# A two-layer diffusion backbone on one core: first-stage statistics, modulation and weight tiles loaded, merged and ordered anew

## The chip, the cores and the metric

The kernel runs on one core of a Trainium2 chip. The metric is the device time of one execution in microseconds, as a median of several. TensorE (PE) does the matrix products and PEld is its weight load; VectorE is DVE, ScalarE is ACT, and SP is the queue that issues every transfer from HBM.

## What is computed

The reference is a backbone of two layers over 512 latent tokens and 256 context tokens with 1024 features. Each layer normalises every token, modulates it, mixes tokens and adds the result under a gate. Only the entry of layer 0 matters here:

```python
def _rms(x):
    return x * lax.rsqrt(jnp.mean(x * x, axis=-1, keepdims=True) + NORM_EPS)

def modulation(cond, mod_w, mod_b):
    m = jax.nn.silu(cond) @ mod_w + mod_b
    return jnp.split(m, 3, axis=-1)     # shift, scale, gate

# a layer: h = _rms(x) * norm_g * (1 + scale) + shift, for latents by c, for context by c_ctx
u = h @ w_in                            # 1024 x 4096, first product of the mixer
```

All arithmetic is in float32. A product of two float32 matrices is made of three passes over halves of reduced mantissa (hi and lo).

## The kernel before, in words

Features lie on partitions, in eight tiles of 128 (k = 0 to 7); tokens lie along the free axis, 256 of the context first (`acc_c`) and 512 latents after them (`acc_l`), 768 in all. A feature tile of the modulated input h is a pair (`hh`, `hl`), a weight tile of 128 by 1024 is split into (`whi`, `wlo`), on ACT for hi and on DVE for lo (`split_w`, L85 to L93). `mm3` (L75 to L78) issues the three products lo by hi, hi by hi and hi by lo. `mm_in` (L279) makes one output tile of 128 channels: for each k six matmuls of 384 tokens, three in each half.

The first stage (L246 to L381) has this order in the program:

- Transfers, all on SP, in this order: the constants (L60); x in four pieces of two feature tiles, context before latents in each (L247, L248); then in turn the first three weight tiles and the modulation weights of f = 0, 1, 2, with a weight tile ahead of each (L291 to L296). A modulation tile is 1 MB and has four buffers; f = 3 to 7 are fetched in the loop (L374).
- 48 products of ones keep PE at work until the statistics come (`warm_up`, L302).
- Statistics: ACT squares all eight feature tiles (L306, L307), DVE adds them up one by one (L309). For each block of 128 tokens a matmul with one moving column sums over partitions (`token_sums`, L198), apart for context and latents; ACT takes the square root and DVE the reciprocal (L204, L205). `token_spread` (L209) multiplies by the identity so that each partition holds 1/rms of every token in PSUM, and ACT copies that to `rstd` in SBUF (L319).
- Modulation of one feature tile f: `mod_mm(f)` is 16 small matmuls (L328) and a copy of the rows to SBUF (L332); `mod_out(f)` sums the rows with a matmul (L172) and DVE makes shift and gain (L338, L343). `mod_mm(0)` is held back behind the last spread (L353).
- `normed(k)` is x by `rstd` on DVE (L348, L349). `make_h` makes `hh` on ACT (L223), the same in full precision (`tmp`, on DVE L225 or on ACT L227), and `hl` as their difference on DVE (L228).
- The loop over k: make h for k, then `mod_mm(k+1)` and `normed(k+1)`, then `mm_in` for k of three output tiles (two of the branch that is convolved, one gate), with `mod_out(k+1)` after the first of them. So the modulation runs one feature tile ahead. At k = 0 the second and third weight tiles are split whole (`take(3, 2)`, L366), after h of k = 0; at k = 3 a softplus of 40 columns is computed.

Program order is a priority, not a fixed order: a scheduler at compile time puts the instructions of each engine in order by its own estimate, and `issue_after` forces one instruction behind another. At run time every engine takes its instructions in that fixed order. After the stage come sixteen iterations of layer 0 and then layer 1; the change does not touch them.

An fp32 matmul that is not of reduced mantissa appears as two instructions in the trace: 50 products of ones are 100 rows, and one `mod_mm` is 32.

Of the kernel before, what the change touches and what calls it, by code (L numbers as in the profile page):

```python
# [7 lines left out]
F32 = mybir.dt.float32  # L8
# [35 lines left out]
def backbone(ctx: ExitStack, tc: tile.TileContext, xT, vec, trig, lru_mod_sc, lru_mod_gt, lru_w_in, lru_w_g, lru_w_out,  # L44
# [171 lines left out]
    def cut(pair, a, b):  # L216
        return [t[:, a:b] for t in pair]
# [16 lines left out]
    with ExitStack() as l0:  # L234
# [14 lines left out]
        nc.scalar.activation(out=cond[:, :, 0:2], in_=vt[:, V_COND:V_COND + 16].rearrange("p (k t) -> p k t", t=2),  # L249
                             func=AF.Silu)  # L250
        segs = ((0, NC), (NC, NT))
# [27 lines left out]
        def mm_in(w, ps, ks=range(KD)):  # L279
            for k in ks:  # L280
                wk = [t[:, k * P:(k + 1) * P] for t in w]
                for a, b in halves:
                    mm3(ps[:, 128 + a:128 + b], wk, cut(hs[k], a, b), k == 0, k == KD - 1)

        with tc.tile_pool(name="mp", bufs=4) as mp, tc.tile_pool(name="mp1", bufs=1) as mp1:
# [16 lines left out]
            warm_up(48)  # L302
            ssum = e("ssum")
            for k in range(KD):
# [6 lines left out]
            parts = [(ssum[:, a:b], slots[1][:, 512 * i:512 * i + 4], (slots[0], slots[2])[i][:, 512:512 + b - a], rstd[:, a:b], b - a)  # L311
                     for i, (a, b) in enumerate(segs)]
# [10 lines left out]
            def mod_mm(f):  # L323
                raw = mraw.pop(f)
                for k in range(KD):
# [20 lines left out]
            def normed(k):  # L346
                t = e("nx")
                nc.vector.tensor_tensor(out=t[:, 0:NC], in0=acc_c[:, k, :], in1=rstd[:, 0:NC], op=ALU.mult)  # L348
                nc.vector.tensor_tensor(out=t[:, NC:NT], in0=acc_l[:, k, :], in1=rstd[:, NC:NT], op=ALU.mult)  # L349
                return t  # L350

            split_to(0)
            with tc.issue_after(spread.ins):  # L353
                rows = mod_mm(0)
            mod_out(0, rows)
            warm_up(4)
            us[0], gps, us[1] = slots[0], slots[1], slots[2]
            nx = normed(0)
            for k in range(KD):
# [4 lines left out]
                if k == 0:  # L364
                    with tc.issue_after(last_lo[0].ins), tc.issue_after(last_hi[0].ins):
                        w3 = take(3, 2)  # L366
# [5 lines left out]
                if k + 1 < KD:  # L372
                    if k + 3 < KD:
                        mraw[k + 3] = mod_load(k + 3)  # L374
                    rows = mod_mm(k + 1)
                    nx = normed(k + 1)
                mm_in(w3[0], us[0], [k])
                if k + 1 < KD:
                    mod_out(k + 1, rows)
                mm_in(w3[1], gps, [k])  # L380
                mm_in(w3[2], us[1], [k])  # L381
# [576 lines left out]
```

## Time and profile before

| | us |
|---|---|
| median of 3 executions | 1082.06 |
| lowest and highest | 1081.18, 1083.04 |
| the profiled execution, its own time | 1082.99 |
| its span from the first to the last instruction | 1081.2 |
| PE, DVE and ACT busy in the span | 1058.2, 706.8, 573.0 |
| granted TensorE clock, mean | 0.994 |

Times in rows are counted from the start of the span. In a row of the timeline the first number is the start and the second the duration, both in microseconds; several equal instructions in a row are merged (x12), and what stands in brackets is the idle time of the engine before it and what ended it. A clock of 1.00 is 2.4 GHz and 0.50 is 1.2 GHz. The ends of matmuls are modelled: where they follow each other, the distance of their starts is the better price.

### The profile page before, as it was taken

What the parts mean: (1) busy time and instruction counts of PE and PEld (TensorE: products, weight loads), DVE (VectorE), ACT (ScalarE), POOL (GpSimd) and SP (SyncE); (2) the same over time, 40 slices, a digit from 0 to 9 for tenths busy, and PEclk for the clock granted to TensorE, in tenths of its full rate; (3) what the DMA queues carried; (4) which work ended last, traced back from release to release, by engine and by line L of the source; (5) the groups of instructions that cost most, each with busy time, mean ns of one, the idle gap of its engine ahead of it and who ended that gap; (6) DMA issues with size and microseconds to landing.
All of it is one profiled execution on the core that took longest, in us unless ns stands there. A gap on an engine that the chain in (4) does not pass through costs nothing.

```text
span 1081.2 us, 15148 instructions
## 1 busy us (share of the span) xinstructions
PE 1058.2 (98%) x6284; PEld 965.0 (89%) x6284; DVE 706.8 (65%) x991; ACT 573.0 (53%) x745; POOL 1.1 (0%) x5
## 2 busy tenths in 40 slices
PE   8999999999999999999999999999999999999996
PEld 7898789999999999998889988899888988889886
DVE  4777667886788777878989755462555525544256
ACT  5557778766687468788366343132432324222254
POOL 0000000000000000000000000000000000000000
PEclk9999999999999999999999999999999999999998
DMA  9524653221222121222113512311122112231102
GB/s 361 220 73 154 205 169 115 69 71 66 69 69 65 53 67 41 78 71 77 68 40 118 195 39 78 98 59 39 59 77 79 59 39 63 74 98 41 39 1 79
DMA packets 29045, 95.56 MB, mean 88 GB/s; under 512 B 2992, under 2 KB 6192, under 8 KB 27952
## 3 DMA queue, kind: packets, MB, share of 16 engines
q1 hardware_dynamic: 28976, 94.59, 26.8%
q8 instruction: 49, 0.80, 0.3%
q14 instruction: 20, 0.16, 0.0%
HBM read 92.48 MB, written 2.10 MB: 87 GB/s over the span
## 4 chain that ended last, share of the span: by engine, by line
PE 64%; ACT 7%; DVE 6%; issue 2%; DVEq 0%
PE ps L76 21%; PE ps L77 21%; PE ps L78 21%; ACT g L468 1%; ACT a L467 1%; DVE xl L264 1%; DVE g L486 1%; ACT q L470 1%; ACT L483 1%; ACT L467 1%; ACT g L452 1%; DVE q L499 1%; DVE q L492 1%; DVE q L498 1%; ACT q L483 1%
## 5 line engine op out<-in xcount | busy, mean ns | idle before, releaser
L76 PE MATMUL ps<-hl,whi 128*128 128x384 f32 (+2 forms) x816 | 286.3, 351 | 1.6 <-DVE hl L228 1.4
L78 PE MATMUL ps<-hh,wlo 128*128 128x384 f32 (+2 forms) x816 | 283.3, 347 | 0.1
L77 PE MATMUL ps<-hh,whi 128*128 128x384 f32 (+2 forms) x816 | 282.9, 347 | 0.0
L91 ACT ACTIVATE whi<-wraw 128x1024 fp32r<-128x1024 f32 (+1 forms) x125 | 125.0, 1001 | 216.9 <-PE ps L77 174.0
L92 DVE TENSOR_TENSOR wlo<-wraw,whi 128x1024 fp32r<-128x1024 f32 (+1 forms) x126 | 145.1, 1153 | 95.6 <-ACT whi L91 75.0
L76 PEld LDWEIGHTS ps<-hl,whi 128*128 128x128 f32 x816 | 153.5, 188 | 18.8 <-issue 3.5
L78 PEld LDWEIGHTS ps<-hh,wlo 128*128 128x128 f32 x816 | 153.4, 188 | 11.0 <-issue 0.8
L77 PEld LDWEIGHTS ps<-hh,whi 128*128 128x128 f32 x816 | 153.5, 188 | 10.3 <-issue 1.0
L76 PE MATMUL ps<-yl,whi 128*128 128x384 f32 (+2 forms) x416 | 143.6, 345 | 3.9 <-DVE yl L501 2.1
L78 PE MATMUL ps<-yh,wlo 128*128 128x384 f32 (+2 forms) x416 | 142.6, 343 | 0.0
L77 PE MATMUL ps<-yh,whi 128*128 128x384 f32 (+2 forms) x416 | 142.5, 343 | 0.0
L77 PE MATMUL ps<-whi,hh 128*128 128x256 f32 x384 | 108.7, 283 | 0.0
L78 PE MATMUL ps<-whi,hl 128*128 128x256 f32 x384 | 108.6, 283 | 0.0
L76 PE MATMUL ps<-wlo,hh 128*128 128x256 f32 x384 | 108.6, 283 | 0.0
L76 PEld LDWEIGHTS ps<-yl,whi 128*128 128x128 f32 x416 | 78.3, 188 | 11.7 <-DVE yl L501 2.9
L78 PEld LDWEIGHTS ps<-yh,wlo 128*128 128x128 f32 x416 | 78.3, 188 | 5.7
L77 PEld LDWEIGHTS ps<-yh,whi 128*128 128x128 f32 x416 | 78.3, 188 | 5.5
L77 PEld LDWEIGHTS ps<-whi,hh 128*128 128x128 f32 x384 | 73.7, 192 | 0.3
L76 PEld LDWEIGHTS ps<-wlo,hh 128*128 128x128 f32 x384 | 73.7, 192 | 0.3
L78 PEld LDWEIGHTS ps<-whi,hl 128*128 128x128 f32 x384 | 73.7, 192 | 0.0
L452 ACT ACTIVATE g<-ps,vt 128x768 f32<-128x768 f32 x64 | 56.2, 897 | 9.1 <-PE ps L78 8.9
L264 DVE SCALAR_TENSOR_TENSOR xl<-ps,vt,xl 128x255 f32<-128x255 f32 (+1 forms) x96 | 54.3, 605 | 0.0
(190 smaller groups left out, 1553.9 us busy)
## 6 DMA issues: line engine op xcount, KB each, us to landing
wraw<-in_ret_w_in_dram SPq DMA_DIRECT2D x48, 512.0 KB, 3.5
wraw<-in_lru_w_in_dram SPq DMA_DIRECT2D x32, 512.0 KB, 3.7
mraw<-in_lru_mod_sc_dram SPq DMA_DIRECT2D x8, 1024.0 KB, 8.8
wraw<-in_ret_mod_w_dram SPq DMA_DIRECT2D x16, 512.0 KB, 4.8
wraw<-in_lru_w_out_dram SPq DMA_DIRECT2D x16, 512.0 KB, 3.5
wraw<-in_ret_w_out_dram SPq DMA_DIRECT2D x16, 512.0 KB, 3.6
wraw<-in_lru_w_g_dram SPq DMA_DIRECT2D x16, 256.0 KB, 2.7
wraw<-in_lru_mod_gt_dram SPq DMA_DIRECT2D x8, 512.0 KB, 4.2
```

What stands on the lines that cost most here:

```text
L76: nc.tensor.matmul(ps, lhsT=lhs[0], rhs=rhs[1], start=first, stop=False)
L77: nc.tensor.matmul(ps, lhsT=lhs[0], rhs=rhs[0], start=False, stop=False)
L78: return nc.tensor.matmul(ps, lhsT=lhs[1], rhs=rhs[0], start=False, stop=last)
L91: nc.scalar.activation(out=hi, in_=raw, func=AF.Copy)
L92: nc.vector.tensor_tensor(out=lo, in0=raw, in1=hi.bitcast(F32), op=ALU.subtract)
L264: nc.vector.scalar_tensor_tensor(out=t[:, o0:o1], in0=u[:, o0 + sh:o1 + sh], scalar=cw[j], in1=t[:, o0:o1], op0=ALU.mult, op1=ALU.add)
L452: nc.scalar.activation(out=t, in_=ps[:, 128:896], func=AF.Sigmoid, bias=vt[:, boff:boff + 1])
L467: nc.scalar.activation(out=a, in_=r, func=AF.Exp, scale=sneg[:, d * CT + c:d * CT + c + 1])
L468: nc.scalar.activation(out=r, in_=r, func=AF.Tanh, scale=spos[:, d * CT + c:d * CT + c + 1])
L470: nc.scalar.activation(out=q, in_=a, func=AF.Square)
L483: nc.scalar.activation(out=q, in_=q, func=AF.Sqrt)
L486: nc.vector.tensor_tensor(out=i, in0=i, in1=q, op=ALU.mult)
```

## The change

1. Transfers: the modulation weights f = 0 come before the first weight tile, f = 1 before the second and third, and f = 2 and 3 after them. Of the last piece of x the latents come before the context. The weights of f + 4 are fetched as soon as `mod_mm(f)` is issued.
2. A square root of one element is put behind the SiLU at the start, so that its table is loaded there.
3. Statistics: only six feature tiles are added up on DVE. The latents of tiles 6 and 7 are squared on ACT, their context on DVE, and both are summed by PE directly: 18 one-column matmuls (6 for the six tiles, 4 + 4 for the latents of tiles 6 and 7, 2 + 2 for their context) and one matmul by zeros that opens the sum, where 6 were before. All six token blocks lie in one 6-column tile, so there is one square root and one reciprocal. `mod_mm(0)` stands between the two spreads in the program and is no longer held back by an `issue_after`. 44 products of ones, none later.
4. `normed(0)` reads the spread from PSUM; the copies to `rstd` come after h of k = 0.
5. The three weight tiles are split in two parts, the first 128 columns (all that k = 0 needs) and the other 896; the heads early, the rests among the matmuls of k = 0.
6. The modulation and `make_h` run two feature tiles ahead of the matmuls.

Cut to its core:

```diff
-            nc.sync.dma_start(out=acc_c[:, k:k + 2, :], in_=xv[:, k:k + 2, 0:NC])
-            nc.sync.dma_start(out=acc_l[:, k:k + 2, :], in_=xv[:, k:k + 2, NC:NT])
+            for a, sl in ((acc_c, slice(0, NC)), (acc_l, slice(NC, NT)))[::-1 if k == 6 else 1]:
+                nc.sync.dma_start(out=a[:, k:k + 2, :], in_=xv[:, k:k + 2, sl])
...
+        with tc.issue_after(silu.ins):
+            nc.scalar.activation(out=warm, in_=eps, func=AF.Sqrt)
...
+            mraw = {0: mod_load(0)}
             fetch_to(0)
-            mraw = {0: mod_load(0)}
-            fetch_to(1)
             mraw[1] = mod_load(1)
             fetch_to(2)
-            mraw[2] = mod_load(2)
+            mraw[2], mraw[3] = mod_load(2), mod_load(3)
...
-            warm_up(48)
+            warm_up(44)
...
-            for k in range(KD):
+            for k in range(6):
...
+            sq6, sq7 = e("sq6"), e("sq7")
+            for k, sq in ((6, sq6), (7, sq7)):
+                nc.scalar.activation(out=sq[:, NC:NT], in_=acc_l[:, k, :], func=AF.Square)
+            for k, sq in ((6, sq6), (7, sq7)):
+                nc.vector.tensor_tensor(out=sq[:, 0:NC], in0=acc_c[:, k, :], in1=acc_c[:, k, :], op=ALU.mult)
...
-            for sq, pt, _, _, n in parts:
-                token_sums(pt, sq, n)
-            warm_up(2)
-            rts = [token_rstd(pt, n, D)[0] for _, pt, _, _, n in parts]
-            for rt, (_, _, ps, rs, n) in zip(rts, parts):
-                spread = token_spread(ps, rt, n)
-                nc.scalar.activation(out=rs, in_=ps, func=AF.Copy)
+            tok = slots[1][:, 0:6]
+            parts = [(ssum, t) for t in range(6)] + [(sq, t) for sq in (sq6, sq7) for t in range(2, 6)]
+            parts += [(sq, t) for sq in (sq6, sq7) for t in range(2)]
+            none = mp1.tile([P, 6], F32, name="none")
+            nc.vector.memset(none, 0.0)
+            nc.tensor.matmul(tok, lhsT=ones, rhs=none, start=True, stop=False)
+            for n, (sq, t) in enumerate(parts):
+                nc.tensor.matmul(tok[:, t:t + 1], lhsT=sq[:, t * P:(t + 1) * P], rhs=ones[:, 0:1], start=False,
+                                 stop=n == len(parts) - 1)
+            rt = mp1.tile([P, 6], F32, name="rt6")
+            nc.scalar.activation(out=rt, in_=tok, func=AF.Sqrt, scale=1.0 / D, bias=eps)
+            nc.vector.reciprocal(out=rt, in_=rt)
+            rsp = [slots[0][:, 512:512 + NC], slots[2][:, 512:1024]]
...
+            def w_part(i, sl):
+                if i == len(w3):
+                    w3.append((wp.tile([P, 1024], F32R, tag="whi", name="whi"), wp.tile([P, 1024], F32R, tag="wlo", name="wlo")))
+                raw, (hi, lo) = raws[i][0], w3[i]
+                nc.scalar.activation(out=hi[:, sl], in_=raw[:, sl], func=AF.Copy)
+                nc.vector.tensor_tensor(out=lo[:, sl], in0=raw[:, sl], in1=hi[:, sl].bitcast(F32), op=ALU.subtract)
...
+            head, rest = slice(0, P), slice(P, 1024)
+            rows = {}
+            token_spread(rsp[0], rt[:, 0:2], NC)
+            rows[0] = mod_mm(0)
+            w_part(0, head)
+            token_spread(rsp[1], rt[:, 2:6], NL)
+            nx = normed(0, rsp)
+            mod_out(0, rows[0])
+            rows[1] = mod_mm(1)
+            us[0], gps, us[1] = slots[0], slots[1], slots[2]
+            dst = [us[0], gps, us[1]]
+            make_hs(0, nx)
+            for a, b, ps in ((NC, NT, rsp[1]), (0, NC, rsp[0])):
+                with tc.issue_after(last_hi[0].ins):
+                    nc.scalar.activation(out=rstd[:, a:b], in_=ps, func=AF.Copy)
+            with tc.issue_after(last_lo[0].ins):
+                w_part(1, head)
+                nx = normed(1)
+                w_part(0, rest)
+            mark = mm_in(w3[0], dst[0], [0])
+            with tc.issue_after(mark.ins):
+                mod_out(1, rows[1])
+            make_hs(1, nx)
+            nx = normed(2)
+            mm_in(w3[1], dst[1], [0])
+            w_part(2, head)
+            mm_in(w3[2], dst[2], [0])
+            w_part(1, rest)
+            rows[2] = mod_mm(2)
+            w_part(2, rest)
+            for k in range(1, KD):
+                if 3 <= k < 6:
+                    rows[k + 2] = mod_mm(k + 2)
+                mm_in(w3[0], dst[0], [k])
+                if k == 1:
+                    mod_out(2, rows[2])
+                    make_hs(2, nx)
+                    nx = normed(3)
+                elif k == 2:
+                    mod_out(3, rows[3])
+                    make_hs(3, nx)
+                    nx = normed(4)
+                elif k < 6:
+                    mod_out(k + 2, rows[k + 2])
+                mm_in(w3[1], dst[1], [k])
+                if k == 2:
+                    rows[4] = mod_mm(4)
+                mm_in(w3[2], dst[2], [k])
+                if k == 1:
+                    rows[3] = mod_mm(3)
+                elif k == 2:
+                    mod_out(4, rows[4])
+                if 2 <= k < 6:
+                    make_hs(k + 2, nx)
+                    if k < 5:
+                        nx = normed(k + 3)
...
```

## Rows read from the trace of the kernel before

**Rows 1.** Busy time, share of the span and instructions of each engine

```profile
PE 1058.2 (98%) x6284; PEld 965.0 (89%) x6284; DVE 706.8 (65%) x991; ACT 573.0 (53%) x745; POOL 1.1 (0%) x5
```

**Rows 2.** Busy time by stretch: start:end, length, busy (instructions), PEclk, DMA share, GB/s

```profile
18.00:19.00 1.00, 0.52 (x2) 0.53 (x3) 0.33 (x2) 0.38 (x2) 0.00 (x0) 0.50 0.97 401
...
15.00:25.90 10.90, 7.80 (x98) 6.90 (x98) 6.43 (x15) 6.12 (x11) 0.00 (x0) 0.84 1.01 416
```

**Rows 3.** Timeline of ACT and DVE up to the end of the statistics

```profile
3.36 1.28 ACT L249 ACT_TABLE_LOAD   x1 [3.36 <-DMA vt<-in_vec_dram]
4.65 0.22 ACT L249 ACTIVATE cond<-vt 128x16 f32<-128x16 f32 x1
...
7.36 0.63 ACT L307 ACTIVATE ssum<-acc_l 128x512 f32<-128x512 f32 x1 [1.88 <-DMA acc_l<-in_xT_dram]
...
13.64 1.15 ACT L307 ACTIVATE sq<-acc_l 128x512 f32<-128x512 f32 x2 [0.33 <-DMA acc_l<-in_xT_dram]
...
10.10 6.27 DVE L309 TENSOR_TENSOR ssum<-ssum,sq 128x768 f32<-128x768 f32 x6 [0.60 <-ACT sq L307]
```

**Rows 4.** Timeline of PE and its weight loads up to the first matmul of the stage

```profile
1.05 12.98 PE L300 MATMUL ps<-ones 128*128 128x128 f32 x100 [1.05 <-DVE ones L64]
16.42 1.41 PEld L198 LDWEIGHTS ps<-ones,ssum 128*128 128x128 f32 x12 [2.59 <-DVE ssum L309]
...
18.48 2.93 PE L209 MATMUL ps<-vt,rt 128*128 128x128 f32 x12 [0.55 <-DVE rt L205]
21.34 1.08 PE L328 MATMUL ps<-mraw,cond 128*32 128x128 f32 x32
22.35 0.71 PE L300 MATMUL ps<-ones 128*128 128x128 f32 x4
...
25.91 0.45 PE L76 MATMUL ps<-hl,whi 128*128 128x384 f32 x1 [1.13 <-DVE hl L228]
```

**Rows 5.** Timeline of ACT and DVE from the sums to the first h

```profile
17.96 0.42 ACT L204 ACTIVATE rt<-ps,eps 128x2 f32<-128x2 f32 x2 [0.69 <-PE ps L198]
...
21.45 0.60 ACT L319 ACTIVATE rstd<-ps 128x512 f32<-128x512 f32 x1 [1.32 <-PE ps L209]
22.07 0.69 DVE L349 TENSOR_TENSOR nx<-acc_l,rstd 128x512 f32<-128x512 f32 x1 [1.50 <-ACT rstd L319]
...
23.45 0.23 DVE L343 TENSOR_SCALAR g<-m,vt 128x2 f32<-128x2 f32 x1
...
23.71 1.31 ACT L223 ACTIVATE hh<-nx,m,g 128x256 fp32r<-128x256 f32 x2 [0.94 <-DVE g L343]
...
25.17 0.68 DVE L228 TENSOR_TENSOR hl<-tmp,hh 128x512 fp32r<-128x512 f32 x1
...
26.37 1.22 DVE L92 TENSOR_TENSOR wlo<-wraw,whi 128x1024 fp32r<-128x1024 f32 x1
```

**Rows 6.** Periods of k = 0, 3, 4, 5: length, PE busy, PEclk, DMA

```profile
25.90:31.30 5.40, 5.03 (x52) 1.00 0.88 363
40.75:46.02 5.27, 4.87 (x55) 1.00 0.78 307
46.02:50.37 4.35, 4.35 (x53) 1.00 0.00 1
50.37:55.10 4.73, 4.65 (x56) 1.00 0.34 115
```

**Rows 7.** Waits of the weight load from 26 to 62 us: total, times, longest

```profile
PEld ps L76 <- DVE hl L228: 3.2, 6, 1.4
```

**Rows 8.** Row sum of f = 1, one-column sums at the end, normalising in layer 1

```profile
27.08 0.28 PE L172 MATMUL ps<-vt,rows 128*128 128x4 f32 x2
...
1063.80 0.50 PE L198 MATMUL ps<-ones,fs 128*128 128x1 f32 x4
1064.16 0.36 PE L76 MATMUL ps<-yl,whi 128*128 128x256 f32 x1
...
L538 DVE TENSOR_TENSOR nx<-acc_l,ps 128x512 f32<-128x512 f32 x8 | 5.5, 681 | 0.0
```

More of the change, by code (lines that the diff above doesn't have):

```diff
@@ L246, in backbone @@
         for k in range(0, KD, 2):
-            nc.sync.dma_start(out=acc_c[:, k:k + 2, :], in_=xv[:, k:k + 2, 0:NC])
-            nc.sync.dma_start(out=acc_l[:, k:k + 2, :], in_=xv[:, k:k + 2, NC:NT])
-        nc.scalar.activation(out=cond[:, :, 0:2], in_=vt[:, V_COND:V_COND + 16].rearrange("p (k t) -> p k t", t=2),
+            for a, sl in ((acc_c, slice(0, NC)), (acc_l, slice(NC, NT)))[::-1 if k == 6 else 1]:
+                nc.sync.dma_start(out=a[:, k:k + 2, :], in_=xv[:, k:k + 2, sl])
+        silu = nc.scalar.activation(out=cond[:, :, 0:2], in_=vt[:, V_COND:V_COND + 16].rearrange("p (k t) -> p k t", t=2),
                              func=AF.Silu)
+        with tc.issue_after(silu.ins):
+            nc.scalar.activation(out=warm, in_=eps, func=AF.Sqrt)
         segs = ((0, NC), (NC, NT))
@@ L282, in mm_in @@
                 for a, b in halves:
-                    mm3(ps[:, 128 + a:128 + b], wk, cut(hs[k], a, b), k == 0, k == KD - 1)
+                    m = mm3(ps[:, 128 + a:128 + b], wk, cut(hs[k], a, b), k == 0, k == KD - 1)
+            return m
         with tc.tile_pool(name="mp", bufs=4) as mp, tc.tile_pool(name="mp1", bufs=1) as mp1:
@@ L309, in backbone @@
                     nc.vector.tensor_tensor(out=ssum, in0=ssum, in1=sq, op=ALU.add)
-            rstd = mp1.tile([P, NT], F32, name="rstd")
-            parts = [(ssum[:, a:b], slots[1][:, 512 * i:512 * i + 4], (slots[0], slots[2])[i][:, 512:512 + b - a], rstd[:, a:b], b - a)
-                     for i, (a, b) in enumerate(segs)]
-            for sq, pt, _, _, n in parts:
-                token_sums(pt, sq, n)
-            warm_up(2)
-            rts = [token_rstd(pt, n, D)[0] for _, pt, _, _, n in parts]
-            for rt, (_, _, ps, rs, n) in zip(rts, parts):
-                spread = token_spread(ps, rt, n)
-                nc.scalar.activation(out=rs, in_=ps, func=AF.Copy)
+            sq6, sq7 = e("sq6"), e("sq7")
[3 more added lines that the diff above has]
+                nc.vector.tensor_tensor(out=sq[:, 0:NC], in0=acc_c[:, k, :], in1=acc_c[:, k, :], op=ALU.mult)
+            rstd = mp1.tile([P, NT], F32, name="rstd")
+            tok = slots[1][:, 0:6]
[11 more added lines that the diff above has]
+            rsp = [slots[0][:, 512:512 + NC], slots[2][:, 512:1024]]
             bank = [slots[3][:, 0:512], slots[3][:, 512:1024]]
@@ L324, in mod_mm, with mod_mm_ @@
                 raw = mraw.pop(f)
+                try:
+                    return mod_mm_(f, raw)
+                finally:
+                    if f + 4 < KD:
+                        mraw[f + 4] = mod_load(f + 4)
+            def mod_mm_(f, raw):
                 for k in range(KD):
@@ L344, in mod_out, with normed, make_hs @@
                                                scalar2=vt[:, V_LG + f:V_LG + f + 1], op0=ALU.add, op1=ALU.mult)
-            def normed(k):
+            def normed(k, rs=(rstd[:, 0:NC], rstd[:, NC:NT])):
                 t = e("nx")
-                nc.vector.tensor_tensor(out=t[:, 0:NC], in0=acc_c[:, k, :], in1=rstd[:, 0:NC], op=ALU.mult)
-                nc.vector.tensor_tensor(out=t[:, NC:NT], in0=acc_l[:, k, :], in1=rstd[:, NC:NT], op=ALU.mult)
-                return t
[L352 to L359, printed above, removed]
+                nc.vector.tensor_tensor(out=t[:, 0:NC], in0=acc_c[:, k, :], in1=rs[0], op=ALU.mult)
+                nc.vector.tensor_tensor(out=t[:, NC:NT], in0=acc_l[:, k, :], in1=rs[1], op=ALU.mult)
+                return t
+            w3 = []
+            def w_part(i, sl):
[4 more added lines that the diff above has]
+                nc.vector.tensor_tensor(out=lo[:, sl], in0=raw[:, sl], in1=hi[:, sl].bitcast(F32), op=ALU.subtract)
+            def make_hs(k, nx):
                 tmp = e("tmp")
@@ L363, in backbone @@
                 make_h(cut(hs[k], NC, NT), NL, nx[:, NC:NT], g0[:, k, 0:1], m0[:, k, 0:1], tmp[:, NC:NT], k == 0)
-                if k == 0:
-                    with tc.issue_after(last_lo[0].ins), tc.issue_after(last_hi[0].ins):
-                        w3 = take(3, 2)
+            head, rest = slice(0, P), slice(P, 1024)
[4 more added lines that the diff above has]
+            token_spread(rsp[1], rt[:, 2:6], NL)
@@ L371, in backbone @@
                         nc.vector.tensor_scalar(out=spos, in0=sp[:, 0:32], scalar1=LRU_C, scalar2=None, op0=ALU.mult)
[L372 to L381, printed above, removed]
+            ready += w3
+            raws[0:3] = [None] * 3
+            pos[0] = 3
         yp = l0.enter_context(tc.tile_pool(name="yp", bufs=7, reuse_waits="tile"))
```

## The prediction

> **What bounds the kernel now.** I read the share of busy time first: PE is busy in 98% of the span [rows 1], so time can only come out of places where PE waits or does extra work. Then the busy time by stretch: from 15 to 25.9 us PE is busy for 7.8 of 10.9 us, and the mean clock is 0.84, with half clock from 18 us [rows 2]. The change lies there and in the 34 us behind it. The timeline of PE gives the head: ones until 14.03, a wait of 2.4 us for the sums, sums, spreads, modulation, and the first matmul of the stage at 25.91 [rows 4]. Everything later hangs on that matmul, so what the head and the stage give up moves the rest of the program.
>
> The chain of the head, step by step: six more additions on DVE run back to back from 10.10 to 16.37, 1.045 us each, while the last squares are ready at 14.79 [rows 3]; so DVE, not HBM, sets the end of the statistics. The 12 one-column instructions take 1.41 us, 0.1175 each, as long as their weight loads [rows 4]; square root at 17.96, spread from 18.48 [rows 4, 5]. The spread takes 12 instructions from 18.48 to 21.34, 0.24 each, at half clock [rows 2, 4]. Then the copy to SBUF (0.60), the latents' product (0.69), and with the gain ready at 23.68 the 2.2 us until h is there [rows 5].
>
> In the stage one period of k is 4.35 us where nothing waits (k = 4: busy 4.35) and no row sum falls in it [rows 6]; a row sum adds 0.28 [rows 8]. Period 0 took 5.40 instead of 4.63 (0.77 lost), period 3 with two row sums 5.27 instead of 4.91 (0.36), period 5 4.73 instead of 4.63 (0.10) [rows 6, 7]. Two more like period 5, and the sum is 1.4 us that running ahead can recover; of the 3.2 us that weight loads wait for h [rows 7], most is under a preceding matmul.
>
> **The change part by part.**
>
> *Transfers.* x is all there at about 13.6 [rows 3]. At 416 GB/s [rows 2] a 1 MB tile takes 2.5 us and a weight tile 1.25: by this estimate modulation 0 lands at 16.2, weight tile 0 at 17.4, modulation 1 at 19.9, weights 1 and 2 at 21.2 and 22.4, modulation 2 and 3 at 25 and 27.5. Nothing below asks for one earlier. On SP the tiles f = 4 to 7 wait for `mod_mm` 0 to 3, all over by 33 us, so the weight tile queued behind them is not later than now. Latents before context in the last piece: squares of latents ready by 14.2 instead of 14.79. Worth nothing by themselves.
>
> *Table of the square root.* It moves from the head, where it hid under the sums, to 4.87 us. In the row the first ACTIVATE starts 0.01 us after a load of 1.28 [rows 3], so squares start 1.5 us later, at 6.4, and the two pairs that could run (0.8) are over before the latents arrive at 7.36. Zero.
> The Trainium skill (ScalarE: Activation LUTs, What ACT_TABLE_LOAD costs) charges a drain of 1.38 us beside the load; by that estimate the squares would come about 1 us later, the additions would end 0.5 us later and the sum below would lose 0.5 us. The row shows no such gap.
>
> *Statistics.* Five additions end at 10.10 + 4 x 1.045 = 14.28, against 16.37: 2.09 earlier. The context squares of tiles 6 and 7 (about 0.4 each, from 0.69 for twice the columns [rows 5]) end by 15.1, before PE wants them. But PE now does 36 one-column instructions where 12 were: 36 x 0.1175 = 4.23, from 14.33 to 18.56, plus 0.1 to drain, against 17.93 [rows 4]. This step alone loses 0.7. Bounds for one: 0.09, as among the dense matmuls at the end of the kernel (1063.80 to 1064.16 for four) [rows 8], which would give back 1.0, and 0.24 at half clock, as a spread. I take 0.1175, the same instruction in the same place.
>
> *Root, spread, modulation 0.* Root and reciprocal stay 0.52 from sum to spread [rows 4, 5]. `mod_mm(0)` has its weights by 16.2 and nothing holds it, so the scheduler can put it into that wait; it takes 1.01 us on PE (21.34 to 22.35) [rows 4]. The spread costs 12 x 0.12 = 1.44 at full clock. PE: 18.56 + 1.01 + 1.44 = 21.0, and 21.1 with the drain, against 21.41. Here the clock decides: I take full clock, because PE's wait shrinks from 2.4 us to 1.5 (44 products of ones end near 12.7) and that of the root is filled; the other end is a rival.
>
> *No copy to SBUF.* The product reads PSUM at 0.68, the same as from SBUF (layer 1 does so) [rows 5, 8]; the 0.60 goes. It runs from 21.15 to 21.83. Shift, gain and the context's h are ready by then, so what is left is the latents' hh (about 0.8 of the pair's 1.31, for two thirds of its columns), hl (0.68) and three hand-overs (0.12): **first matmul at 23.4, against 25.91: 2.5 gained.** `mod_mm(1)` fits into PE's wait before it. The copies to `rstd` follow on ACT (0.9 us), before PE reaches the bank that they read.
>
> *Stage.* Matmuls, six `mod_mm` and seven row sums after the first matmul stay as they were. DVE gets new work in the first two periods: the rests of three weight tiles (7/8 of 1.22 each [rows 5], 3.2 us, of which one tile was split in the head before), two products, two h. With the heads and gains that is about 9 us in two periods of 4.63 each: it fits, with hardly any slack. h of k = 2 is the tightest: its gain comes behind those rests at about 30.2, then hh of both parts (1.31), the latents' tmp on ACT (as long as their hh, 0.8) and hl (0.68) lead to about 33.0, where PE comes at 32.65 after two periods of 4.63: 0.35 lost. From k = 3 on, h is a whole period ahead and the softplus no longer hurts. Other bounds: none lost, or 1.9 if the head of weight tile 2 stands behind the product for k = 2 on DVE (PE wants its lo 2.4 us after the first matmul; behind it comes 1.5 later). I take 0.35. **Net 1.4 - 0.35 = 1.05 gained.**
>
> *Sum.* 2.5 + 1.05 = 3.55 us. The profiled execution took 1082.99 (span 1081.2), 0.93 over the median of 1082.06. Against its own time that is 1079.4, on the median 1078.5, and I give the middle, **1079.0 us**, since I don't know whether the other executions had the stretch at half clock. A measurement of this kernel can tell about 0.2%, 2.2 us, from no change.
>
> **Rivals.**
>
> *A: the order leaves holes.* The scheduler keeps `mod_mm(0)` between the spreads, as the program has it. Then rows and row sum of f = 0 come behind the latents' spread: spread of context 19.2 to 19.7, modulation to 20.7, spread to 21.7, row sum to 22.0, gain at 22.85 behind the product, then the 2.2 us as now: first matmul at 25.1, a gain of 0.85. With 0.35 to 1.9 lost in the stage against the 1.4 recovered, 0.3 to 1.9 in all: 1080.2 to 1082.7. For it: a priority by program order, and a DVE queue that is nearly full in period 0. Against it: PE has nothing else to do in the 0.52 between the sums and the spread, and the modulation's weights are there.
>
> *B, the other side: the clock.* Sums with one moving column may not hold TensorE's clock up. For it: PE did only sums in the stretch before the clock fell at 18.0 [rows 2, 4], and now 4.2 us of such sums stand behind a wait. If it falls as they begin, each costs 0.24: 36 x 0.12 = 4.4 more, the spread 1.44 more, the modulation about 1.0 more by the same ratio; first matmul at 30.3, 4.4 later than now, and with 1.05 recovered the kernel is 3.3 slower: 1085.4 on the median. The point: the 3.55 are gone once the spread and the modulation (2.4) and about 9 of 36 sums run at half clock; slower by 2.2 us needs some 28 of them, that is a fall before 15.4 us. A fall at 18.0, as before, leaves a small gain of about 0.5: 1081.6. Against it: PE is busy without a break from 14.3 on.
> The Trainium skill (TensorE: Matmul & The Clock Gate, What's actually happening) says that a monitor sets the clock by how busy PE has been; by that the sums, busy without a break, would keep it up, and the trace, with sums in only part of the stretch before the fall, does not settle it.
>
> *C: the two tiles ahead do not come about,* because the scheduler orders by its own estimate and DVE has no slack before k = 3. Then only the head gains: about 2, 1080.5. I count it with A.
>
> **How the numbers follow.** Forecast 0.55 (0.52 faster by over 0.2%, 0.03 same), A with C 0.27 (0.05 faster, 0.21 same, 0.01 slower), B 0.18 (0.08 same, 0.10 slower). Faster 0.57, same 0.32, slower 0.11. The range goes from 1076.6 (1078.5 with no 0.35 lost, sums at 0.09, and 0.5 for the scatter of a median over executions that lie 1.9 us apart) to 1082.7, the far end of A; it leaves out the bad half of B and little else.
>
> **What would show it.** Right: no addition of tiles 6 and 7 on DVE, 36 one-column instructions from about 14.3 to 18.6 at a clock of 1.00, the first matmul of the stage near 23.4, no table load near 16 us, and no wait of a weight load for hl from k = 3 on. Wrong: a clock of 0.50 while the sums run (B), row sum 0 behind the latents' spread (A), or a matmul of k = 0 that waits for the lo of weight tile 2 (A). If the first matmul comes at 23.4 and the time does not fall, something later than the stage sets the time, which PE's 98% speaks against.

## The result, and the profile after

The changed kernel takes **1090.03 us** (median of 4 runs, 1088.91 to 1091.60) against 1082.55 for the kernel before on the same chip (4 runs, 1081.18 to 1083.74): ratio 1.0067, 95% interval 1.0054 to 1.0080. It is 7.5 us slower, where I had forecast 3 us less. The profiled execution took 1091.60, 1.6 over its median, with a span of 1089.8 against 1081.2.

The page of the changed kernel, its span, the busy time of PE and the granted clock in 40 slices of 27 us:

```profile
span 1089.8 us, 15164 instructions
...
PE 1065.4 (98%) x6290; PEld 972.0 (89%) x6290; DVE 706.2 (65%) x994; ACT 572.0 (52%) x746; POOL 1.1 (0%) x5
...
PEclk7799999999999999999999999999999999999999
```

PE's share is 98% as before [rows 1], with 7.2 us more in it (1065.4 against 1058.2), of 8.6 in the span: PE waits only 1.4 us more, it is slower, and only in the first two slices. The busy time by stretch of the changed kernel (us of the stretch, busy us of PE, PEld, DVE, ACT and POOL with instructions, granted clock, DMA share, GB/s):

```profile
14.00:16.00 2.00, 2.00 (x18) 2.00 (x19) 0.59 (x2) 0.00 (x0) 0.00 (x0) 1.00 1.01 406
16.00:17.00 1.00, 1.00 (x8) 1.00 (x7) 0.00 (x0) 0.00 (x0) 0.00 (x0) 0.60 1.04 418
17.00:33.00 16.00, 12.35 (x98) 10.62 (x98) 5.92 (x14) 4.95 (x11) 0.00 (x0) 0.50 0.82 309
33.50:36.50 3.00, 1.39 (x8) 1.07 (x7) 2.93 (x7) 2.55 (x5) 0.00 (x0) 1.00 0.67 279
37.00:43.00 6.00, 5.71 (x44) 4.79 (x44) 1.44 (x3) 0.28 (x2) 0.00 (x0) 0.50 0.16 25
43.50:60.00 16.50, 16.50 (x198) 14.55 (x198) 11.95 (x33) 11.26 (x21) 0.00 (x0) 1.00 0.60 228
```

The clock falls to half (1.2 GHz) just after 16 us, while PE does nothing but one-column sums and has been busy with them for 2.00 of the 2.00 us before. It comes back only after 33 us, for 3 us, and is at half again until 43. The mean clock of all four executions is 0.987 to 0.991, against 0.993 to 0.998 in the ten of a1_wide below, so the fall is not the profiled execution's alone. In the kernel before it was at half from 18.0 to 21.4 us and nowhere else up to 60 us:

```profile
18.00:21.39 3.39, 2.91 (x16) 2.69 (x20) 0.76 (x3) 0.76 (x3) 0.00 (x0) 0.50 1.01 414
21.40:60.00 38.60, 36.45 (x415) 32.15 (x415) 28.11 (x82) 22.48 (x38) 0.00 (x0) 1.00 0.57 217
```

What the half clock does to PE in the changed kernel, in its timeline (start, us, instruction, count, and in brackets the idle time before it and what ended it):

```profile
13.97 1.50 PE L325 MATMUL ps<-ones,ssum 128*128 128x1 f32 x12 [0.38 <-DVE ssum L311]
15.33 4.47 PE L325 MATMUL ps<-ones,sq 128*128 128x1 f32 x24
20.39 2.93 PE L209 MATMUL ps<-vt,rt 128*128 128x128 f32 x12 [0.58 <-DVE rt L329]
23.25 1.94 PE L346 MATMUL ps<-mraw,cond 128*32 128x128 f32 x32
25.58 0.59 PE L172 MATMUL ps<-vt,rows 128*128 128x4 f32 x2 [0.40 <-ACT rows L350]
28.85 0.66 PE L76 MATMUL ps<-hl,whi 128*128 128x384 f32 x1 [2.68 <-ACT rstd L399]
29.43 1.94 PE L346 MATMUL ps<-mraw,cond 128*32 128x128 f32 x32
...
31.79 0.52 PE L78 MATMUL ps<-hh,wlo 128*128 128x384 f32 x1
...
34.27 0.34 PE L78 MATMUL ps<-hh,wlo 128*128 128x384 f32 x1
36.21 0.44 PE L76 MATMUL ps<-hl,whi 128*128 128x384 f32 x1 [1.61 <-ACT whi L376]
...
37.29 0.69 PE L76 MATMUL ps<-hl,whi 128*128 128x384 f32 x1 [0.45 <-DVE hl L228]
...
39.51 1.94 PE L346 MATMUL ps<-mraw,cond 128*32 128x128 f32 x32
```

A sum is here one instruction of the trace, two of which make one of the 18 matmuls. By the trace their starts lie 0.112 us apart up to 16.1, for 20 of the 36, and 0.213 apart for the 16 behind the fall. A modulation product takes 1.94 where it was done in about 1.0 [rows 4]; a matmul of the stage lasts 0.52 where it lasts 0.34 at full clock. The first matmul of the stage comes at 28.85, against 25.91 [rows 4]. Behind it stand three things of the order: `mod_mm(1)` among the matmuls of k = 0, a wait of 1.61 us for the head of weight tile 2, and one of 0.45 for hl of k = 1. ScalarE shows the early table loads and the chain from root to h:

```profile
4.79 1.28 ACT L252 ACT_TABLE_LOAD   x1
6.08 0.20 ACT L252 ACTIVATE warm<-eps 128x1 f32<-128x1 f32 x1
...
19.84 0.27 ACT L328 ACTIVATE rt<-ps,eps 128x6 f32<-128x6 f32 x1 [6.13 <-PE ps L325]
25.25 0.28 ACT L350 ACTIVATE rows<-ps 128x128 f32<-128x128 f32 x1 [5.14 <-PE ps L346]
...
26.67 1.31 ACT L223 ACTIVATE hh<-nx,m,g 128x256 fp32r<-128x256 f32 x2
27.88 0.84 ACT L399 ACTIVATE rstd<-ps 128x512 f32<-128x512 f32 x2
...
35.16 0.80 ACT L227 ACTIVATE tmp<-nx,m,g 128x512 f32<-128x512 f32 x1
35.87 1.14 ACT L376 ACTIVATE whi<-wraw 128x128 fp32r<-128x128 f32 x2
```

And VectorE, for the lines that answer to [rows 3, 5]:

```profile
9.77 4.15 DVE L311 TENSOR_TENSOR ssum<-ssum,sq 128x768 f32<-128x768 f32 x4 [0.41 <-ACT sq L309]
...
23.35 0.69 DVE L367 TENSOR_TENSOR nx<-acc_l,ps 128x512 f32<-128x512 f32 x1 [1.29 <-PE ps L209]
26.21 0.16 DVE L356 TENSOR_TENSOR m<-ps,vt 128x4 f32<-128x4 f32 x1 [2.16 <-PE ps L172]
```

The additions are over at 13.92. The latents' product is done at 24.04, but shift and gain come at 26.21, since the modulation runs behind both spreads: rival A's hole.

To see where the loss stops I use one mark, the first convolution on ScalarE (`xl<-ps`), which needs the first of the stage's three output tiles whole. It starts at 70.50, before at 61.98: 8.52 later, and the span is 8.6 longer. So all of it is lost in this stage: 2.94 us ahead of the first matmul (28.85 - 25.91), and 5.58 between it and the mark (41.65 against 36.07).

The mark does not stand at the same place of PE's order in all kernels. With the loop of the kernel before (before, a3, a4, b_wide) 145 matmuls of 384 columns have begun ahead of it, with the changed loop 138, which is 7 x 0.173 = 1.2 us less work. Counted over the same 144 matmuls, from the first to the start of the 145th, the stage takes 35.95 us before and 42.74 in the changed kernel, 6.79 more:

```profile
25.91:61.86 35.95, 34.93 (x351) 31.22 (x352) 24.83 (x74) 20.26 (x35) 0.00 (x0) 1.00 0.48 180
28.85:71.59 42.74, 40.69 (x382) 35.90 (x383) 27.75 (x79) 22.32 (x39) 0.00 (x0) 0.87 0.38 136
```

PE is idle in them for 1.02 and 2.05 us, and busy for 5.76 more. Of these some 1.0 (its price at full clock [rows 4]) is `mod_mm(1)`, which stood ahead of the first matmul before; the other 4.8 are by this estimate the price of half clock in the stage.

### The profile page after: what moved, and what is told of

It is laid out like the page before. It is cut to its first block, busy times and chain, and to the rows that moved or that the text cites. A ratio compares the mean times of both kernels' runs of the same rounds, so it can differ in the third digit from the quotient of the medians.

```text
span 1089.8 us, 15164 instructions
## 1 busy us (share of the span) xinstructions
PE 1065.4 (98%) x6290; PEld 972.0 (89%) x6290; DVE 706.2 (65%) x994; ACT 572.0 (52%) x746; POOL 1.1 (0%) x5
## 4 chain that ended last, share of the span: by engine, by line
PE 64%; ACT 7%; DVE 6%; issue 2%; DVEq 0%
PE ps L76 21%; PE ps L77 21%; PE ps L78 21%; ACT g L535 1%; ACT a L534 1%; DVE xl L266 1%; DVE g L553 1%; ACT q L537 1%; ACT L550 1%; ACT L534 1%; ACT g L519 1%; DVE q L566 1%; DVE q L559 1%; DVE q L565 1%; ACT q L550 1%
## 5 line engine op out<-in xcount | busy, mean ns | idle before, releaser
L91 ACT ACTIVATE whi<-wraw 128x1024 fp32r<-128x1024 f32 (+1 forms) x122 | 121.9, 1000 | 220.4 <-PE ps L77 177.7
L92 DVE TENSOR_TENSOR wlo<-wraw,whi 128x1024 fp32r<-128x1024 f32 (+1 forms) x123 | 141.4, 1151 | 96.6 <-ACT whi L91 76.0
```

The lines of the kernel that those rows point to most:

```text
L91: nc.scalar.activation(out=hi, in_=raw, func=AF.Copy)
L92: nc.vector.tensor_tensor(out=lo, in0=raw, in1=hi.bitcast(F32), op=ALU.subtract)
```

## The experiments

Theory: one-column sums back to back let the clock fall, and the half clock outlasts them. Rivals: the new order alone costs the time (A), the wait of PE ahead of the sums drops the clock, or the change is worth nothing even without these. "64 columns" below means that each sum is multiplied by 64 equal columns of ones and one of the 64 results is read; nothing of the computation is left out. Ratios are against the kernel before on the same chip (medians 1082.55 to 1083.75). All figures but the medians and ratios are from one profiled execution each, in us; x lands up to 0.9 us earlier or later from one execution to the next, and the times of the head shift with it.

| kernel | median | ratio to before, 95% | first matmul | mark | from one to the other |
|---|---|---|---|---|---|
| before | 1082.55 | | 25.91 | 61.98 | 36.07 |
| changed | 1090.03 | 1.0067 [1.0054, 1.0080] | 28.85 | 70.50 | 41.65 |
| a1_wide | 1082.41 | 0.9994 [0.9984, 1.0003] | 25.06 | 60.36 | 35.30 |
| a2_oldstat | 1083.73 | 1.0006 [0.9994, 1.0017] | 27.52 | 63.27 | 35.75 |
| a3_newstat_only | 1088.49 | 1.0055 [1.0033, 1.0077] | 27.89 | 67.11 | 39.22 |
| a4_newstat_wide | 1082.99 | 0.9997 [0.9988, 1.0007] | 25.18 | 61.28 | 36.10 |
| b_wide | 1082.93 | 1.0001 [0.9992, 1.0010] | 24.63 | 61.00 | 36.37 |
| s1_head | 1083.19 | 1.0003 [0.9994, 1.0012] | 23.57 | 61.23 | 37.66 |
| s2_stage | 1080.01 | 0.9976 [0.9966, 0.9986] | 24.43 | 59.04 | 34.61 |
| s2_onecol | 1087.57 | 1.0039 [1.0027, 1.0052] | 27.89 | 65.61 | 37.72 |
| s3_oldstat | 1079.40 | 0.9966 [0.9952, 0.9981] | 23.29 | 57.89 | 34.60 |
| s3_stageonly | 1081.00 | 0.9980 [0.9966, 0.9994] | 24.65 | 59.28 | 34.63 |
| s4_fill | 1083.56 | 1.0004 [0.9989, 1.0018] | 28.73 | 62.54 | 33.81 |

**a1_wide**: the changed kernel with 64 columns.

```diff
-            tok = slots[1][:, 0:6]
+            tok = slots[1][:, 0:384]
...
-            none = mp1.tile([P, 6], F32, name="none")
+            none = mp1.tile([P, 384], F32, name="none")
...
-                nc.tensor.matmul(tok[:, t:t + 1], lhsT=sq[:, t * P:(t + 1) * P], rhs=ones[:, 0:1], start=False,
+                nc.tensor.matmul(tok[:, 64 * t:64 * (t + 1)], lhsT=sq[:, t * P:(t + 1) * P], rhs=ones[:, 0:64], start=False,
...
-            nc.scalar.activation(out=rt, in_=tok, func=AF.Sqrt, scale=1.0 / D, bias=eps)
+            nc.scalar.activation(out=rt, in_=tok.rearrange("p (t c) -> p t c", c=64)[:, :, 0], func=AF.Sqrt, scale=1.0 / D, bias=eps)
```

> The changed kernel with 64 equal moving columns in each of its 18 sums in place of one (only the first column is read). Theory 1 (sums with one moving column let TensorE's clock fall, and the fall is the loss): the clock stays at 1.00 from 12 to 30 us, a sum costs the same 0.11 to 0.12 us per instruction, the first matmul of the stage comes at 24 to 25 instead of 28.85, and the time is 1078 to 1081. Theory 2 (the loss is the order: weight heads and the modulation of f = 1 stand in the way, whatever the clock): the clock holds, the time stays at 1086 or more. The order of the engines also changes a little here, since the compile-time estimate of a wide sum is longer, so a fall to 1081 alone does not part clock from order. Theory 3 (the wait of PE before the sums drops the clock): the clock falls all the same.

The product by zeros that opens the sum becomes wider too, 384 columns in place of 6. That is not what holds the clock: b_wide and s3_oldstat below have no such product, s4_fill has the narrow one, and all three keep 1.00.

Measured: 7.6 us less than the changed kernel, level with the kernel before. Stretches of a1_wide, then its timeline of PE:

```profile
12.00:20.00 8.00, 7.75 (x77) 7.03 (x79) 2.94 (x6) 1.96 (x5) 0.00 (x0) 1.00 1.01 410
20.00:25.06 5.06, 2.99 (x69) 2.46 (x57) 3.38 (x10) 3.29 (x8) 0.00 (x0) 1.00 1.03 427
25.06:31.71 6.65, 5.15 (x52) 3.99 (x53) 6.59 (x14) 4.42 (x9) 0.00 (x0) 1.00 0.90 356
31.71:60.00 28.29, 28.20 (x290) 25.73 (x291) 19.82 (x64) 16.24 (x28) 0.00 (x0) 1.00 0.43 158
```

```profile
15.56 2.84 PE L325 MATMUL ps<-ones,sq 128*128 128x64 f32 x24
...
25.06 0.41 PE L76 MATMUL ps<-hl,whi 128*128 128x384 f32 x1 [1.34 <-ACT rstd L399]
...
31.71 0.44 PE L76 MATMUL ps<-hl,whi 128*128 128x384 f32 x1 [1.23 <-DVE hl L228]
```

The clock is 1.00 throughout, and a sum with 64 columns costs what one with one column does at full clock (0.112). The scheduler's order is not that of the changed kernel, though only the width was edited: `mod_mm(1)`, for one, is back ahead of the first matmul. What is left is rival A: first matmul at 25.06 (A: 25.1), and a period 0 of 6.65 us in which VectorE is busy for 6.59: three rests of weight tiles (started at 25.77, 27.04 and 29.97) stand in its queue ahead of the latents' hl of k = 1.

**a2_oldstat**: the changed kernel with the statistics of the kernel before (seven additions, 12 one-column sums).

```diff
-            for k in range(6):
+            for k in range(KD):
...
+            for sq, pt, _, _, n in parts:
+                token_sums(pt, sq, n)
```

> The changed kernel with the statistics of before (eight tiles squared on ACT and added on DVE, 6 sums, 50 products of ones, two roots), all else as changed. Theory 1: half clock lasts about 3 us as before, the first matmul comes near 25.5, the time is 1080 to 1083. Theory 2: 1086 or more.

Measured: no difference from before that can be told. The clock is at half in two pieces, from 17.5 to 24.3 and from 27.7 to 31.1 us, 10.2 us in all where I expected about 3, and the first matmul comes at 27.52, not near 25.5; the 12 sums begin at 16.61. Taking 24 of the 36 sums out gives back most of the loss, not the half clock as a whole.

**a3_newstat_only** and **a4_newstat_wide**: the kernel before with the new statistics alone (the same block of the change, followed by the old spread, copies and order), and that with 64 columns as in a1_wide.

> The kernel before with the new statistics alone (six tiles added, 18 one-column sums after a zero matmul, 44 products of ones, one root; the other 4 products of ones stay, transfers, splits and loop as before). Theory 1: the clock is at half for most of 16 to 33 us, the first matmul comes at 28 or later, the time is 1085 to 1090. Theory 2: 1082 to 1084, since the order of the loop is that of before.

> The previous kernel with 64 moving columns in each sum. Theory 1: the clock holds at 1.00 through the sums, the first matmul comes at 25 to 26 and the time is 1080 to 1083, 4 or more below the one with one column. Theories 2 and 3: no more than 1 us from the one with one column.

Measured: 1088.49 and 1082.99. Only the width was edited between these two, so the 5.5 us are the width of the sums and what it does to the order. On PE one piece stands elsewhere: `mod_mm(1)` comes behind the third matmul of the stage with one column and ahead of the first with 64 (on ScalarE and VectorE a few weight splits change places). Of the 2.71 us between their first matmuls it has no part; of the 3.12 between the first matmul and the mark it is about 1.0 at full clock. Stretches of a3_newstat_only, then of a4_newstat_wide:

```profile
18.00:24.00 6.00, 5.42 (x49) 4.82 (x48) 2.44 (x4) 2.19 (x4) 0.00 (x0) 0.50 1.01 418
...
28.50:31.00 2.50, 2.50 (x36) 1.59 (x34) 1.07 (x1) 0.00 (x0) 0.00 (x0) 0.50 0.12 46
```

```profile
14.00:30.00 16.00, 13.87 (x170) 12.29 (x174) 10.46 (x23) 9.86 (x16) 0.00 (x0) 1.00 1.02 419
```

So the new statistics carry most of the loss by themselves, without the new transfers, splits and loop.

**b_wide**: the kernel before with 64 columns in its own 12 sums.

```diff
-                token_sums(pt, sq, n)
+                for t in range(n // P):
+                    nc.tensor.matmul(pt[:, t:t + 64], lhsT=sq[:, t * P:(t + 1) * P], rhs=ones[:, 0:64], start=True, stop=True)
```

> The kernel before with 64 equal columns in its 12 sums of this stage, nothing else changed. It had half clock from 18.0 to 21.4 us, over the spread and the modulation. If its one-column sums were the reason: clock 1.00 there, the spread at 0.13 in place of 0.24 each, the first matmul at about 24.2 in place of 25.91, and 1.5 us less, about 1081.5. If the wait of 2.4 us ahead of the sums was the reason: the same half clock and the same time as before, 1083.

Measured: the half clock from 18.0 to 21.4 is gone (1.00 from 14 to 60 us) and the first matmul comes 1.28 earlier, yet the time is the same and not 1.5 us less. The wait ahead of the sums is shorter here, 1.20 us against 2.40, since the products of ones end later, so this pair alone doesn't part width from wait; s3_oldstat below, with wide sums behind a wait of 1.82, keeps 1.00. 0.30 is lost again up to the mark, and the rest behind it. The stretch from 60 to 200 us of the kernel before, then of b_wide:

```profile
60.00:200.00 140.00, 139.09 (x793) 122.00 (x794) 103.10 (x132) 101.16 (x119) 0.00 (x0) 1.00 0.46 149
```

```profile
60.00:200.00 140.00, 138.11 (x786) 120.73 (x786) 102.82 (x131) 100.75 (x119) 0.00 (x0) 1.00 0.46 149
```

PE is idle there for 0.98 us more, of which 0.5 is one longer wait for the transfer of a later modulation tile (1.0 in place of 0.5) and 0.5 a wait for `xl` that was not there before. In these two executions an earlier start of one microsecond is not passed on in full.

**s1_head**: a1_wide with the head in the order that the prediction counted on.

```diff
-            token_spread(rsp[0], rt[:, 0:2], NC)
             rows[0] = mod_mm(0)
+            token_spread(rsp[0], rt[:, 0:2], NC)
             w_part(0, head)
+            mod_out(0, rows[0])
...
-            mod_out(0, rows[0])
```

> The run with wide sums (64 equal columns) and the head's order put as the prediction had it: the first modulation product in the wait for the square root, the head of weight tile 0 and the gain of f = 0 ahead of the spread of the latents' tokens. If the order of the head took the rest of the gain: the spread of the latents ends near 21.0 us as before, normed(0) no longer waits for the gain, and the first matmul of the stage starts at about 23.4 us in place of 25.06; the time falls by about 1.6 us against the run with wide sums alone, to about 1080.8. If the copies of the scale factors on ScalarE (0.84 each) set the first matmul whatever the order: it starts at 24.6 or later and the time stays at 1082. The clock stays at 1.00 in both cases.

Measured: the first matmul comes at 23.57, as foreseen, and the time does not fall. Timeline of PE, then the stretch behind it:

```profile
23.57 0.41 PE L76 MATMUL ps<-hl,whi 128*128 128x384 f32 x1 [1.58 <-ACT rows L350]
...
28.21 0.44 PE L76 MATMUL ps<-hl,whi 128*128 128x384 f32 x1 [1.62 <-ACT whi L376]
...
29.15 0.61 PE L76 MATMUL ps<-hl,whi 128*128 128x384 f32 x1 [0.33 <-DVE hl L228]
```

```profile
29.00:32.00 3.00, 2.85 (x22) 2.36 (x26) 1.30 (x3) 0.00 (x0) 0.00 (x0) 0.54 0.51 202
```

The head of weight tile 2 is made on ScalarE behind hh and tmp of k = 1, as in the changed kernel; PE waits 1.62 us for it, and then the clock is at half for some 3 us. What the head gained the stage gave back.

**s2_stage**: s1_head with the order of the first two periods put by hand too.

```diff
             with tc.issue_after(last_lo[0].ins):
                 w_part(1, head)
+                w_part(2, head)
+                g_1 = mod_out(1, rows[1])
                 nx = normed(1)
+            with tc.issue_after(g_1.ins):
                 w_part(0, rest)
...
+            with tc.issue_after(last_lo[0].ins):
+                w_part(1, rest)
+                w_part(2, rest)
+                nx = normed(2)
```

> The same with the order of the first two periods put by hand too: the heads of weight tiles 1 and 2 and the gain of f = 1 ahead of the first matmul, the rests of tiles 1 and 2 and the product for k = 2 behind the hl of k = 1. If the three rests on VectorE ahead of the h of k = 1 are what stretched period 0 to 6.65 us: period 0 falls to about 4.7 us, the clock stays at 1.00, and the time is 1.5 to 2 us under the run with the head's order alone, about 1079, faster than the kernel before by 0.3 to 0.4%. If VectorE has too much to do in the first two periods in any order: period 0 shortens, period 1 or 2 lengthens by as much, and the time stays within 0.5 us of the run with the head's order alone.

Measured: 2.6 us less than before, the first version that is faster. Period 0 is 24.43 to 28.90, 4.47 us, with a wait of 0.45 for the head of weight tile 2 in place of 1.62, and the clock is 1.00 throughout. Compared with the 6.65 of a1_wide, about 1.0 of the difference has only moved: a modulation product fell into period 0 there, and falls into period 1 here.

```profile
24.43 0.41 PE L76 MATMUL ps<-hl,whi 128*128 128x384 f32 x1 [1.58 <-ACT rows L350]
...
27.46 0.45 PE L76 MATMUL ps<-hl,whi 128*128 128x384 f32 x1 [0.45 <-ACT whi L376]
...
28.90 0.45 PE L76 MATMUL ps<-hl,whi 128*128 128x384 f32 x1
```

(Its x landed 0.85 us later than in s1_head, hence 24.43 and not 23.57.)

**s2_onecol**: the same edits with one-column sums (the width of a1_wide put back).

> The same edits of the order with one-column sums as in the changed kernel. If the width of the sums decides the clock: half clock from about 16 us on, the first matmul at 27 us or later, and 5 to 8 us more than with wide sums, 1085 to 1088. If it was the changed kernel's order (its gaps on TensorE behind the sums) that kept the clock down: a half clock of no more than 3.4 us, and within 2 us of the run with wide sums.

Measured: 7.6 us more than s2_stage. The clock falls at 16.9 us, during the sums, and is at half to 23.7 and again from 27.1 to 34.0. The scheduler gives this kernel, as the changed one, the spreads ahead of `mod_mm(0)`, so the pair differs in order as well as in width; a3 and a4 are the cleaner pair.

**s3_oldstat**: s2_stage with the statistics of b_wide (seven additions, 12 sums of 64 columns) in place of the new ones.

> The kernel with wide sums, head and stage reordered, but with the statistics of the kernel before (seven additions on VectorE, 12 sums, 64 equal columns each). If the new statistics lose 0.2 to 0.7 us of the head whatever the clock, as the sum of the prediction had it: the square root comes 0.2 to 0.6 us earlier than with the new statistics (measured from the landing of the latents), and the time is the same or up to 0.7 us less, about 1079.5 to 1080. If the new statistics are what the gain came from: 1 us or more above the kernel with wide sums, head and stage reordered, 1081 or more.

Measured: 3.4 per mille under before, the fastest of all, and not above s2_stage. With the clock held, the new statistics bring nothing: from the first square of the last latents to the square root it is 5.13 us here (12.82 to 17.95) and 5.65 in s2_stage (13.44 to 19.09), 0.52 less as expected. a4_newstat_wide against b_wide says the same (5.08 and 4.40).

**s3_stageonly**: a1_wide with the edits of the stage alone. The gain then comes behind the latents' product.

> Wide sums and the reordered stage, with the program order of the head as in the changed kernel; by the order the scheduler gives, TensorE's row sum of f = 0 comes behind the spread of the latents' tokens and the gain behind their normed product, the rest as in the kernel with head and stage reordered. If the gain behind the product costs the first matmul 0.5 us and nothing else: first matmul 0.4 to 0.7 us later than there from the landing of the latents, time 1080.5. If the head's order is worth as much as the stage's: 1081.5 or more.

Measured: 1081.00, between the two cases. The stage's order takes the length from first matmul to mark to 34.63 by itself, as in s2_stage. The head's order is worth more at the first matmul than I expected of it: from the start of the square root to the first matmul it is 6.62 us here (18.03 to 24.65), as in a1_wide, and 5.35 in s1_head (18.22 to 23.57), 1.27 more and not 0.4 to 0.7, since with the gain behind the product both parts of h and the copies of the scale factors queue up on ScalarE behind it. In the whole time little of that is left: the ratios to before are 0.9980 here and 0.9976 in s2_stage, and their intervals overlap.

**s4_fill**: the changed kernel, one-column sums and all, with a 128-column product of ones behind each of the 18 matmuls of the sums; its result is not read.

```diff
-                nc.tensor.matmul(tok[:, t:t + 1], lhsT=sq[:, t * P:(t + 1) * P], rhs=ones[:, 0:1], start=False,
-                                 stop=n == len(parts) - 1)
+                m = nc.tensor.matmul(tok[:, t:t + 1], lhsT=sq[:, t * P:(t + 1) * P], rhs=ones[:, 0:1], start=False,
+                                     stop=n == len(parts) - 1)
+                with tc.issue_after(m.ins):
+                    nc.tensor.matmul(slots[2][:, 0:P], lhsT=ones, rhs=ones, start=True, stop=True)
```

> The changed kernel with its one-column sums, and a 128-column product of ones behind each of the 18 sums (36 more instructions on the path). If one-column sums back to back are what lets the clock fall: clock 1.00 through the sums, 36 x 0.115 = 4.1 us more of them, they end at about 22.5 us, first matmul near 29, and the time is 1086 to 1087, LESS than the changed kernel's 1090 although work was added. If something else in the changed kernel takes the clock down (the wait ahead of the sums, the transfers, the zero product): half clock from about 16 us as in the changed kernel, and the added products come on top, 1094 or more.

Measured: 36 instructions of work added on the path, and 6.5 us less than the changed kernel. The stretch of the sums, and the first matmul in the timeline of PE:

```profile
13.98:22.20 8.22, 8.22 (x72) 8.11 (x72) 0.62 (x2) 0.20 (x2) 0.00 (x0) 1.00 1.02 416
```

```profile
28.73 0.44 PE L76 MATMUL ps<-hl,whi 128*128 128x384 f32 x1 [1.44 <-ACT rstd L401]
```

The clock stays at 1.00. The first matmul is as late as in the changed kernel (28.73 and 28.85), but the mark comes at 62.54 and not at 70.50: the stage behind it runs at full clock (33.81 against 41.65). This is some 3 us better than expected; a later first matmul finds its weights split and `mod_mm(1)` done, which I take for the reason. The scheduler also placed the modulation otherwise here, so the 8 us are the clock and what the order added to it. Counted over the same 144 matmuls PE is busy for 34.36 us here and for 40.69 in the changed kernel, and idle for 0.54 and 2.05.

## Why the prediction was wrong

**The step that failed** is "Here the clock decides: I take full clock, because PE's wait shrinks". The case behind it, rival B, came true: the clock fell, in the sums, at 16.2 us. Its counter-argument, that PE is busy without a break from 14.3 us on, held as a fact (2.00 of 2.00 us) and did not help. The pairs a3 and a4, before and b_wide, the changed kernel and a1, and s4_fill show that it is the one-column instructions back to back: the same sums with 64 columns, or with a wide product behind every two, keep 1.00 while they run. The wait ahead of the sums is not it: s2_stage (0.55 us idle there), a4 (0.98) and s3_oldstat (1.82) have no fall, the changed kernel (0.38) has one. The Trainium skill (TensorE: Matmul & The Clock Gate, What's actually happening) lets the clock follow how busy PE has been; what I read from it, that sums without a break keep the clock up, the stretch from 14 to 17 us refutes.

**B's price was too low**, 3.3 us against 7.5. In the head it was too high: 20 of the 36 sums ran before the fall, and the other 16 cost 0.213 each, not 0.24, so the first matmul came at 28.85, not 30.3. But it let the half clock end with the head and the stage recover 1.05. In fact the clock stayed at half to 33.3, well into k = 0, and again from 36.7 to 43.5, and the stage took 5.58 us more up to the mark, 6.79 over the same matmuls. The point "a fall before 15.4" went with it: a fall at 16 was enough.

**The order**: the range's other case, A, was also true. The scheduler did not put `mod_mm(0)` into the root's wait, put `mod_mm(1)` into k = 0, and left the head of weight tile 2 behind hh and tmp. With the clock held (a1_wide) what is left of this order alone eats the gain: first matmul 25.06, period 0 of 6.65, 1082.41.

**What held.** The early table load costs nothing: the next ACTIVATE starts 0.01 us after it (4.79 + 1.28, 6.08), so the drain that the Trainium skill charges (ScalarE: Activation LUTs, What ACT_TABLE_LOAD costs) does not show. The additions end at 13.92 (14.28 predicted), a sum costs 0.112 at full clock (0.1175), and the new statistics lose 0.52 and 0.68 us (0.7), by s2_stage against s3_oldstat and by a4 against b_wide.

**What came near by luck.** The head's sum gives 23.4 for the order that it assumed, and s1_head has 23.57, but two misses cancel: the square root starts at 18.22 there, where the sum has 18.66, and from it to the first matmul it is 5.35 us, where the sum has 4.74. The stage's term, 1.4 to recover and 1.05 net, did not come out. From first matmul to mark s2_stage takes 1.46 us less than before, but 1.2 of that is the mark's place; over the same 144 matmuls it is 0.25:

```profile
24.43:60.13 35.70, 34.79 (x350) 31.18 (x351) 27.71 (x79) 22.08 (x38) 0.00 (x0) 1.00 0.53 199
```

PE is idle in them for 0.91 us, before for 1.02: the waits that the plan meant to recover are still there. Only s4_fill, whose late first matmul finds its weights split, takes 34.90 for these matmuls, 1.05 less than before. What the earlier mark gives to the program behind it was not in the sum. So the forecast of 1079.0 comes near what the plan reaches when the clock is held and the order is put by hand (s3_oldstat 1079.40, s2_stage 1080.01), but not by its own terms, and it is not what this change does.

One premise of the first paragraph was too simple: that what the head gives up moves the rest one for one. s1_head came 1.49 us earlier than a1_wide to the first matmul and 0.87 later to the mark; s4_fill came 3.67 later and 2.18 later. The prediction's last sign, a first matmul near 23.4 without a fall of the time, came up in s1_head too, and there the stage itself gave the gain back, not something later.

**Open.** Why the half clock lasted from 16 to 33 us in the changed kernel, when in a3 it came in two pieces of 6.8 and 3.4 and in the kernel before in one of 3.4, no run isolates. Nor is it shown that the second piece, from 36.7 us, belongs to the sums: it stands behind waits of PE of 1.61 and 0.45 us, and in s1_head, with wide sums, the clock fell at 29.3 behind a wait of 1.62 for the same weight tile. In a4_newstat_wide it fell once more at 137.3, behind a wait of 1.14. A wait of 1.58 in s2_stage had no fall behind it.

## What to carry to other kernels

Where a TensorE instruction's price is set by its weight load, give the moving side more columns rather than one: here 64 columns cost nothing (0.112 us either way) and kept the clock. In the kernel before that brought no time (b_wide, ratio 1.0001). When a change puts narrow products back to back, price the half clock on everything behind them, not on them alone, and look at the granted clock by stretch first when a time comes out wrong. Before a gain from moved work is counted, see where the scheduler really puts it in each engine's queue: two tiles ahead in the program was not two tiles ahead on ScalarE and VectorE.

## What the runs showed of the hardware that I had not expected

- Adding 36 instructions of 128 columns among one-column sums took the kernel from a ratio of 1.0067 [1.0054, 1.0080] to 1.0004 [0.9989, 1.0018].
- PE was busy throughout the 2 us before the clock fell from 2.4 to 1.2 GHz; what it did in them was one-column products only.
- At half clock a one-column sum takes 0.213 us in place of 0.112, though it moves one column only; an instruction of the spread, with 128 columns, takes 0.24 in place of 0.13 (12 in 2.93, and in 1.60 in b_wide).
